# Seven half-size products for the two gates and branch b of a hybrid encoder layer, with the gated sum in natural layout

## The chip, the cores and the metric

The program runs on one core of a Trainium2 chip. A core has a matrix engine (TensorE, here PE, with its weight loads as PEld), a vector engine (DVE), a scalar engine (ACT), a general engine (GpSimd, here POOL) and SyncE (SP), which issues most DMAs. POOL issues the DMAs that add to what lies in the on-chip memory. The metric is the time of one execution in microseconds (us); lower is better.

## The reference

There are two layers on 512 tokens of width 1024, in float32. A layer begins with one input projection of x; its columns are the queries, keys and values of two kinds of attention, a gate g for the second kind, and the two branch gates:

```python
proj = x @ w_in[i]
q_na, k_na, v_na, q_r, k_r, v_r, g_r, gate_a, gate_b = jnp.split(proj, IN_SPLITS, axis=-1)
ya = neighbourhood_attention(q_na.reshape(B, T, NA_HEADS, NA_HEAD_DIM), ...)      # 512 x 512
yb = bidirectional_retention(q_r.reshape(B, T, RET_HEADS, RET_QK_DIM), ..., v_r, g_r, ...)   # 512 x 1024
merged = jax.nn.sigmoid(gate_a) * (ya @ w_branch_a[i]) + jax.nn.sigmoid(gate_b) * (yb @ w_branch_b[i])
y = merged @ w_out[i]
x = layer_norm(DEEPNORM_ALPHA * x + y, ln1_g[i], ln1_b[i])
```

Three of these products concern us: x by gate a's weights, x by gate b's weights, and yb by `w_branch_b`. Each is 512 x 1024 by 1024 x 1024. The layer ends with a gated feed-forward part (`w_up`, a convolution of width 3, `w_down`) with an extra gated input, and a second normalisation.

## The kernel before

**Precision.** Each float32 operand is split into a rounded high part and a low part (`split`: ACT makes the high part, DVE subtracts it to get the low part). A product is three matmuls, high by high, high by low and low by high (`mm3`). So each chunk of weights, 128 x 1024 and 512 KB, costs one ACT cast, one DVE subtraction and the DMA that brings it.

**Weights.** The class `Stream` holds the chunks of both layers in the order of use. `get` hands out the next chunk and prepares (`prep`) those a little ahead; `load` issues the DMAs. Chunks whose split parts are `held` lie in the pool `unit` of 30 buffers (4 KB a partition each), the others in small pools.

**Blocks.** Some products are done by Winograd's scheme: the operands are cut into four quarters, and seven products of half size take the place of eight. The products are called a, c, t1, t2, d, t3 and t4. For t1 to t4 the weights are sums of quarters: a chunk already loaded gets another quarter added, by an accumulating DMA from POOL's queue (`add`), or on POOL with a tensor addition where a quarter is on the chip already (`other`). The activations' sums come from DVE (`vg_sums`: t1, t2, d, t3). One product is 24 matmuls of 512 columns. Before the change, v and g of the retention heads (two blocks, 0 and 1, half of the heads each), the extra input's gate, and the down projection are done in this way.

**Stages of a layer.** In the front part, `vg` runs the fourteen products of blocks 0 and 1, in the order that the tuple `VG` lists, and between them four tiles of gate a (`ga0` to `ga3`) and the first query and key head. Each engine runs the instructions of this part in the order in which they are written. Then follows a middle part, in slots: in each slot `fillers` runs one projection tile from the list `FILL` (24 products of 512 columns with `gemm_t`, output features on the partitions), and steps of retention heads (`RET_AT`) and of neighbourhood attention heads (`NA_AT`) stand in front of it at the slots listed. After `FILL`, `gates` runs eight pairs of tiles: gate b and branch b. In this part a planner orders each engine's instructions, by their place in the text and by when they are ready. Gate a is written to memory after its sigmoid and read again in the next stage. Then come branch a's eight tiles, with the gated sum of both branches, split as it stands because features lie on the partitions already; then the output projection with the first normalisation, the extra input's gate with the up and down projection, and the next layer. In the second layer `plain_x` reads x and applies the last normalisation's factors on DVE.

**Names.** `gt` is a tile of `gemm_t`; `ybt` is branch b's transposed input; `lo`, `hi` are weights' parts; `raw`, `rawa`, `rawd`, `rawt` are chunks as they came; `u`, `v`, `w` are blocks' accumulators; `s`, `sh`, `sl` are sums of activations; `S` is an attention head's scores. In the pinned front part and in most of the later stages, all instructions bear line 84, that of the wrapper that pins them.

```python
for m in range(8):                                            # gates(), before
    sab[m] = unit_f("sab", (P, 2, 512))
    nc.scalar.activation(sab[m][:, 1, :], gemm_t(xs), AF.Sigmoid)
    bb = gemm_t(lambda k: (ybt[k][:, 0, :], ybt[k][:, 1, :]))
    nc.vector.tensor_mul(sab[m][:, 1, :], bb, sab[m][:, 1, :])
```

## Time and profile before

| | |
|---|---|
| median of 3 runs (lowest, highest) | 1700.62 us (1700.49, 1700.91) |
| the profiled execution | 1699.88 us, its span 1697.9 us |
| PE, PEld busy | 1681.9 us, 1404.5 us |
| DVE, ACT, POOL busy | 1207.3 us, 948.7 us, 175.3 us |
| DMA | 250.09 MB, mean 147 GB/s |
| granted TensorE clock | 0.998 |

The span runs from the first to the last instruction; the execution's own time has some 2 us around it. A busy time is the union of an engine's instructions. A row of a group gives the line, the engine, the operation, the tiles (out<-in), the shape and the count, then busy time, the mean length of one in ns, the idle time of the engine in front of them, and what ended that idle time. A row of the timeline or of the chain gives the start and the length in us.

### The profile page before, as it was taken

Reading aid. Unit: us, or ns where it says so; the run is one execution under the profiler, and the core shown is the slowest. Engines: PE = TensorE matmul, PEld = TensorE weight load, DVE = VectorE, ACT = ScalarE, POOL = GpSimd, SP = SyncE. Lnnn points to the kernel's source line nnn. Section 1 sums busy time; section 2 is a strip of 40 time slices with the busy share of each in tenths; the row PEclk is TensorE's granted clock in tenths of the full one; section 3 lists DMA queues with packets and bytes.
Section 4 is the critical chain, followed back from the end, with each engine's and each line's share of the span. In section 5 each row is a group of like instructions: output and inputs, shape, how many; then the busy total and the mean of one; then the engine's idle time right before and its main releaser. Section 6 shows DMA issues by size and latency. Waiting matters only on the chain.

```text
span 1697.9 us, 21017 instructions
## 1 busy us (share of the span) xinstructions
PE 1681.9 (99%) x7895; PEld 1404.5 (83%) x7895; DVE 1207.3 (71%) x1816; ACT 948.7 (56%) x1432; POOL 175.3 (10%) x166
## 2 busy tenths in 40 slices
...
GB/s 322 186 104 131 105 151 123 114 171 126 197 149 145 128 112 162 135 111 173 191 216 149 97 112 124 150 124 108 166 179 198 137 169 124 92 179 131 87 211 99
DMA packets 74406, 250.09 MB, mean 147 GB/s; under 512 B 8640, under 2 KB 9152, under 8 KB 74304
## 3 DMA queue, kind: packets, MB, share of 16 engines
...
## 4 chain that ended last, share of the span: by engine, by line
PE 97%; DVE 2%; ACT 1%; issue 0%; DVEq 0%; ACTq 0%
PE gt L84 32%; PE u L84 13%; PE gt L382 8%; PE gt L381 8%; PE gt L383 8%; PE v L84 7%; PE w L84 3%; PE gn L383 3%; PE gn L382 3%; PE gn L381 3%; PE x L84 2%; PE gn L84 1%; PE na L994 1%; PE pt L982 1%; PE o L383 1%; PE o L382 1%
## 5 line engine op out<-in xcount | busy, mean ns | idle before, releaser
L84 PE MATMUL gt<-x1t,hi 128*128 128x512 f32 x1408 | 433.5, 389 | 0.0
L84 PEld LDWEIGHTS gt<-x1t,hi 128*128 128x128 f32 x1408 | 264.3, 188 | 55.0
L84 PE MATMUL gt<-x1t,lo 128*128 128x512 f32 x704 | 274.1, 389 | 0.1
L84 DVE TENSOR_TENSOR lo<-raw,hi 128x1024 fp32r<-128x1024 f32 (+1 forms) x147 | 182.9, 1253 | 30.5 <-ACT hi L84 30.2
L84 DVE SCALAR_TENSOR_TENSOR ca<-gt,cw,ca 128x511 f32<-128x511 f32 x176 | 131.8, 749 | 79.1 <-ACT ca L84 76.0
L84 ACT CAST hi<-raw 128x1024 fp32r<-128x1024 f32 (+1 forms) x147 | 151.2, 1037 | 32.7 <-PE u L84 14.9
L381 PE MATMUL gt<-xt,hi 128*128 128x512 f32 x416 | 163.5, 393 | 0.0
L382 PE MATMUL gt<-xt,hi 128*128 128x512 f32 x416 | 162.2, 390 | 0.0
L383 PE MATMUL gt<-xt,lo 128*128 128x512 f32 x416 | 162.1, 390 | 0.0
L84 PEld LDWEIGHTS gt<-x1t,lo 128*128 128x128 f32 x704 | 132.1, 188 | 28.2 <-DVE lo L84 1.0
L154 DVE TENSOR_TENSOR lo<-raw,hi 128x1024 fp32r<-128x1024 f32 x72 | 87.9, 1222 | 86.0 <-ACT hi L153 73.7
L84 ACT ACTIVATE ca<-gt,cw 128x512 f32<-128x512 f32 x88 | 68.6, 779 | 131.0 <-PE gt L84 131.0
L153 ACT CAST hi<-raw 128x1024 fp32r<-128x1024 f32 x72 | 75.6, 1051 | 107.0 <-PE gt L382 93.2
L84 DVE TENSOR_TENSOR lo<-rawa,hi 128x1024 fp32r<-128x1024 f32 x90 | 104.5, 1174 | 42.8 <-ACT hi L84 42.6
L84 ACT CAST hi<-rawa 128x1024 fp32r<-128x1024 f32 x90 | 89.6, 1012 | 35.5 <-DMA rawa<-in_wpack 16.9
L383 PEld LDWEIGHTS gt<-xt,lo 128*128 128x128 f32 x416 | 78.1, 188 | 16.6
L381 PEld LDWEIGHTS gt<-xt,hi 128*128 128x128 f32 x416 | 78.2, 188 | 15.1
L382 PEld LDWEIGHTS gt<-xt,hi 128*128 128x128 f32 x416 | 78.2, 188 | 14.6
...
L84 PE MATMUL gt<-xt,hi 128*128 128x512 f32 x192 | 59.4, 391 | 2.7 <-ACT hi L84 2.7
L84 PE MATMUL v<-hi,sa 128*128 128x512 f32 x176 | 56.1, 389 | 0.0
L381 PE MATMUL gn<-hi,mt 128*128 128x512 f32 x128 | 50.1, 392 | 0.0
...
## 6 DMA issues: line engine op xcount, KB each, us to landing
raw<-in_wpack SPq DMA_DIRECT2D x239, 512.0 KB, 3.9
rawa<-in_wpack POOLq DMA_DIRECT2D x58, 512.0 KB, 5.9
lo<-in_wpack POOLq DMA_DIRECT2D x24, 512.0 KB, 6.9
rawa<-in_wpack SPq DMA_DIRECT2D x22, 512.0 KB, 6.4
rawt<-in_wpack SPq DMA_DIRECT2D x22, 512.0 KB, 5.7
rawt<-in_wpack POOLq DMA_DIRECT2D x14, 512.0 KB, 6.6
r_scr<-pp SPq DMA_DIRECT2D x8, 512.0 KB, 9.2
rawd<-in_wpack SPq DMA_DIRECT2D x8, 512.0 KB, 7.0
```

The costliest lines, as they stand in the source:

```text
L84: r = f(*a, **k)
L153: nc.scalar.copy(hi, src)
L154: nc.vector.tensor_sub(lo, src, _f(hi))
L381: nc.tensor.matmul(ps, lh, rh, start=start, stop=False, skip_group_check=more)
L382: nc.tensor.matmul(ps, lh, rl, start=False, stop=False, skip_group_check=more)
L383: nc.tensor.matmul(ps, ll, rh, start=False, stop=stop, skip_group_check=more)
L982: nc.tensor.transpose(ps[:, i * P:(i + 1) * P], S[:, g * 256 + bb * P:g * 256 + (bb + 1) * P], ident)
L994: nc.tensor.matmul(ov[kt], lv, pt[kt // 2][:, sp_, c], start=i == 0 and sp_ == 0, stop=i == 3 and sp_ == 1)
```

## The change

- Gate a and gate b become blocks of seven half-size products, numbers 2 and 3, with tokens on the partitions (natural layout), and run in the front part ahead of and among v's and g's blocks. Both gates are written to memory after the sigmoid (`send`, one product later) and read back as whole rows.
- Branch b becomes such a block (`bb`), in the last seven slots of the middle part. A retention head's transposed output is kept in float32 (`Y`); `quad` and `quad_sums` make the operands, in the buffer that held the transposed x and in units. Its outputs are multiplied with gate b as they come (`M`).
- Branch a is computed in natural layout too; the gated sum is turned by transposes on PE (`turn`) for the output projection.
- On-chip additions on POOL: t2 and t3 of blocks 1, 2 and 3 and t3 of block 0. Branch b's sums are all made by accumulating DMAs.
- The softmax scaling of the attention heads goes from ACT to POOL, and the factors of `plain_x` from DVE to POOL.
- The lists of slots and orders become separate for the two layers.

```diff
-FILL = ("q1", "k1", "ga4", "nq0", "nk0", "q2", "ga5", "k2", "ga6", "nq1", "nk1", "q3", "ga7", "k3", "nq2", "nk2", "nq3", "nk3", "vn")
-RET_AT = (0, 5, 9, 15)
-NA_AT = (17, 19, 21, 23, 25, 27, 30, 32)
+FILL = (('nq0', 'q1', 'nk0', 'k2', 'k1', 'vn', 'q2', 'q3', 'k3', 'nq1', 'nk1', 'nq2', 'nq3', 'nk3', 'nk2'),
+ ('k1', 'q1', 'nk0', 'nk2', 'nq0', 'nq1', 'q2', 'q3', 'k2', 'k3', 'vn', 'nk1', 'nq2', 'nk3', 'nq3'))
+BB = ("a", "c", "t1", "d", "t2", "t3", "t4")
+RET_AT = ((5, 6, 13, 14), (3, 5, 11, 11))
+NA_AT = ((6, 11, 14, 16, 18, 19, 19, 19), (10, 13, 16, 16, 16, 19, 19, 19))
...
-VG0 = ("p0", "p1", "0a", "0c", "1a", "1c", "ga0", "0t1", "ga1", "0t2", "ga2", "0d", "0t3", "1t1", "0t4", "ga3", "1t2", "q0", "1d", "1t3", "k0", "1t4")
-VG1 = ("0a", "0c", "1a", "1c", "ga0", "0t1", "ga1", "0t2", "ga2", "0d", "0t3", "1t1", "0t4", "ga3", "1t2", "q0", "1d", "1t3", "k0", "1t4")
-VG = (VG0, VG1)
+VG = (('p0', 'p1', '2a', '3a', '3c', '2c', '2t1', '2t2', '3t1', '2d', '3t2', '2t3', '3d', '1a', '3t3', '3t4', '2t4', '0a', '0c', '1c', '0t1', '0d', 'q0',
+  '0t2', '1t1', '0t3', '0t4', 'k0', '1d', '1t2', '1t3', '1t4'),
+ ('2a', '2c', '3a', '3c', '3t1', '2t1', '3t2', '2d', '3d', '2t2', '0a', '2t3', '3t3', '0c', '2t4', '1a', 'q0', '0t1', '3t4', '0d', '0t2', '1c', '1t1',
+  '1d', '0t3', '0t4', '1t2', 'k0', '1t3', '1t4'))
+XN_AT = 5
+M_AT = 4
+TABLES_AT = (12, 15)
+REST_AT = (1, 3, 5, 8, 10, 12)
+PEND_AT = (2, 3)
...
+ON_CHIP = ('t3', 't2 t3', 't2 t3', 't2 t3')
+BB_HELD = ('a', 't1', 't2')
+BB_EARLY = 'c'
...
+        def bb_items(l):
+            pos = {(q, j): (l, 44 + 2 * i + j, 0, 1024) for i, q in enumerate("acbd") for j in range(2)}
+            by = {}
+            for it in block_items(pos, {k: up for k in BB_HELD}, BB_EARLY):
+                by.setdefault(it.kind, []).append(it)
+            return [it for k in BB for it in by[k]]
...
-                    for f in FILL:
+                    for f in FILL[l]:
                         self.seq += plain_items(l, f)
-                    for c in (*range(36, 52), *range(60, 72)):
+                    self.seq += bb_items(l)
+                    for c in range(60, 72):
...
+            def block(lh, emit):
+                st = {}
+                def product(kind, ps, first):
+                    for j in range(2):
+                        hi, lo = ws.get()
+                        for i in range(2):
+                            for kk in range(2):
+                                k, r = 2 * j + kk, slice(kk * 512, (kk + 1) * 512)
+                                mm3(ps[i], lh(kind, k, 0, i), lh(kind, k, 1, i), hi[:, r], lo[:, r], first and k == 0, k == 3, not first)
+                def copies(ps, name):
+                    out = [tmp(name) for _ in range(2)]
+                    for i in range(2):
+                        nc.scalar.copy(out[i], ps[i])
+                    return out
+                def corner():
+                    if "t2" in st and "d" in st:
+                        for i, t in enumerate(st["t2"]):
+                            nc.vector.tensor_add(t, t, st["v"][i])
+                            emit(i, 1, t, -1.0)
+                def step(kind):
+                    if kind == "a":
+                        st["u"] = two("u")
+                        product(kind, st["u"], True)
+                        st["p1"] = copies(st["u"], "p1")
+                    elif kind == "c":
+                        w = two("w")
+                        product(kind, w, True)
+                        for i, t in enumerate(st["p1"]):
+                            nc.vector.tensor_add(t, t, w[i])
+                        for i, t in enumerate(st["p1"]):
+                            emit(i, 0, t, 1.0)
+                    elif kind == "t1":
+                        st["v"] = two("v")
+                        product(kind, st["v"], True)
+                        p5 = unit_f("p5", (P, 2, 512))
+                        st["p5"] = [p5[:, i] for i in range(2)]
+                        for i in range(2):
+                            nc.scalar.copy(p5[:, i], st["v"][i])
+                    elif kind == "t2":
+                        product(kind, st["u"], False)
+                        st["t2"] = copies(st["u"], "u2")
+                        corner()
+                    elif kind == "d":
+                        product(kind, st["v"], False)
+                        st["d"] = True
+                        corner()
+                    elif kind == "t3":
+                        product(kind, st["u"], False)
+                        for i, t in enumerate(st["p5"]):
+                            nc.vector.tensor_add(t, t, st["u"][i])
+                            emit(2 + i, 1, t, -1.0)
+                    else:
+                        product(kind, st["u"], False)
+                        for i in range(2):
+                            emit(2 + i, 0, st["u"][i], 1.0)
+                    return st
+                return step
+            stores = []
+            def send():
+                while stores:
+                    g, t, hb, src = stores.pop(0)
+                    nc.sync.dma_start(gscr[g][t * P:(t + 1) * P, hb * 512:(hb + 1) * 512], src)
+            def gate(g):
+                def emit(t, hb, src, sign):
+                    dst = tmp("sg") if hb == 0 and t >= 2 else src
+                    nc.scalar.activation(dst, src, AF.Sigmoid, scale=sign)
+                    stores.append((g, t, hb, dst))
+                return emit
...
+            def vg_emit(hp):
+                def emit(t, hb, src, sign):
+                    (g_tile if hb else v_tile)(hp, t, src)
+                return emit
+                blocks = [block(lh, vg_emit(0)), block(lh, vg_emit(1)), block(lh, gate(0)), block(lh, gate(1))]
...
-            def gate_a(m):
-                sg = tmp("sga")
-                nc.scalar.activation(sg, gemm_t(xs), AF.Sigmoid)
-                nc.sync.dma_start(gscr[m], sg)
...
+                q, kp = h // 2, h % 2
+                Y[q, kp] = unit_f("Y", (P, 2, 2, 256))
                 for dv in range(2):
                     ps = bank("ybt")
                     for t in range(4):
                         nc.tensor.transpose(ps[:, t * P:(t + 1) * P], yb[:, t, dv * P:(dv + 1) * P], ident)
-                    u = unit_r("ybt")
-                    split(u[:, 0, :], u[:, 1, :], ps)
-                    ybt[2 * h + dv] = u
+                    nc.scalar.copy(Y[q, kp][:, dv].rearrange("p a b -> p (a b)"), ps)
...
-                for g in range(4):
-                    nc.scalar.activation(S[:, g * 256:(g + 1) * 256], S[:, g * 256:(g + 1) * 256], AF.Copy, scale=rc[:, g:g + 1])
+                s4 = S.rearrange("p (g n) -> p g n", g=4)
+                nc.gpsimd.tensor_tensor(s4, s4, _ap(rc, 0, [[1, 4], [0, 256]]), ALU.mult)
...
-                        nc.vector.tensor_mul(z, z, g)
-                        nc.vector.tensor_add(z, z, b)
-            def gates():
...
+            def bb():
+                yw = xp.tile([P, 8, 2, 512], F32R, tag="xt", name=nm("yw"))
+                xq = [yw[:, i].rearrange("p a b -> p (a b)").rearrange("p (k c) -> p k c", k=4) for i in range(8)]
+                free = {"a": 0, "c": 2, "t1": 4, "t2": 6}
+                alloc = lambda kind: ((xq[free[kind]], xq[free[kind] + 1]) if kind in free else
+                                      tuple(up.tile([P, 4, 256], F32R, tag="u", name=nm("yq")) for _ in range(2)))
+                X = lambda q, h, kp: Y[q, kp][:, :, h, :]
+                S = {}
+                def quad(kind, q, h):
+                    S[kind] = alloc(kind)
+                    for kp in range(2):
+                        r = slice(2 * kp, 2 * kp + 2)
+                        split(S[kind][0][:, r, :], S[kind][1][:, r, :], X(q, h, kp))
+                sums = quad_sums(X, S, alloc)
+                def load_gate():
+                    for t in range(len(M), len(M) + 2):
+                        M.append(unit_f("M"))
+                        nc.sync.dma_start(M[t], gscr[1][t * P:(t + 1) * P, :])
+                def emit(t, hb, src, sign):
+                    m = M[t][:, hb * 512:(hb + 1) * 512]
+                    nc.vector.scalar_tensor_tensor(m, src, sign, m, op0=ALU.mult, op1=ALU.mult)
+                step = block(lambda kind, k, s, i: S[kind][s][:, k, i * P:(i + 1) * P], emit)
+                quad("a", 0, 0)
+                for n, kind in enumerate(BB):
+                    if n == XN_AT:
                         plain_x()
-                    sab[m] = unit_f("sab", (P, 2, 512))
-                    nc.scalar.activation(sab[m][:, 1, :], gemm_t(xs), AF.Sigmoid)
+                    if n in (0, M_AT):
+                        load_gate()
+                    if n == 1:
+                        quad("c", 1, 0)
+                    if 1 <= n < 5:
+                        next(sums)
+                    if n == 4:
+                        quad("t4", 1, 1)
+                    step(kind)
                     yield
...
-            mt = []
-            for m in range(8):
-                if m % 2 == 0:
-                    wa = ws.get()
-                ba = gemm_t(lambda k: (yat[k][:, 0, :], yat[k][:, 1, :]), nk=4, wt=wa, off=(m % 2) * 512)
-                sa, sb = sab[m][:, 0, :], sab[m][:, 1, :]
-                if m % 4 == 0:
-                    for i in range(m, m + 4):
-                        nc.sync.dma_start(sab[i][:, 0, :], gscr[i])
-                nc.vector.tensor_mul(sa, ba, sa)
-                nc.vector.tensor_add(sa, sa, sb)
-                u = unit_r("mt")
-                split(u[:, 0, :], u[:, 1, :], sa)
-                mt.append(u)
+            mt = {(q, h): [up.tile([P, 4, 256], F32R, tag="u", name=nm("mt")) for _ in range(2)] for h in range(2) for q in range(2)}
+            sa = []
+            for t in range(4):
+                sa.append(unit_f("sa"))
+                nc.sync.dma_start(sa[t], gscr[0][t * P:(t + 1) * P, :])
+            def merge(hb, t, ps):
+                c = slice(hb * 512, (hb + 1) * 512)
+                nc.vector.tensor_mul(sa[t][:, c], ps, sa[t][:, c])
+                nc.vector.tensor_add(sa[t][:, c], sa[t][:, c], M[t][:, c])
+            def turn(hb, t):
+                ps = bank("tr")
+                for k in range(4):
+                    nc.tensor.transpose(ps[:, k * P:(k + 1) * P], sa[t][:, (4 * hb + k) * P:(4 * hb + k + 1) * P], ident)
+                ts = slice((t % 2) * P, (t % 2 + 1) * P)
+                hi, lo = mt[hb, t // 2]
+                split(hi[:, :, ts], lo[:, :, ts], ps.rearrange("p (k c) -> p k c", c=P))
+            for hb in range(2):
+                pss = []
+                for t in gemm_n_tok(lambda k, s, t: yat[k][:, s, t * P:(t + 1) * P], 2, pss, 0):
+                    merge(hb, t, pss[t])
+                    if hb:
+                        turn(0, t)
+            for t in range(4):
+                turn(1, t)
...
-    sga, sgb, sbb, sba = _stat(ga), _stat(gb), _stat(w_bb), _stat(w_ba)
-    for m in range(8):
-        ch += [sgb[m], sbb[m]]
-    ch += list(sga)
-    for m in range(0, 8, 2):
-        ch.append(np.concatenate([sba[m], sba[m + 1]], axis=1))
+    for w in (gb, w_bb, ga, w_ba):
+        ch += list(_mov(w).reshape(-1, P, 1024))
```

209 lines of the change are left out of this document (90 added, 119 removed).

## The prediction

> **What bounds the kernel now.** I read the busy times first, then the chain that ended last, then the order of PE's matmuls, then the busy time by stretch. Times are in us unless marked ns.
>
> ```profile
> PE 1681.9 (99%) x7895; PEld 1404.5 (83%) x7895; DVE 1207.3 (71%) x1816; ACT 948.7 (56%) x1432; POOL 175.3 (10%) x166
> PE 97%; DVE 2%; ACT 1%; issue 0%; DVEq 0%; ACTq 0%
> 99.83 0.39 PE L84 MATMUL u<-lo,sh 128*128 128x512 f32 x1
> 100.06 0.39 PE L84 MATMUL u<-hi,sl 128*128 128x512 f32 x1
> 594.62 87.04 PE gt L84 x384
> ```
>
> The chain that ended last is PE for 97% of the span. A matmul over 512 columns lasts 0.39, but the next starts 0.23 later: 384 of them in a row take 87.04, which is 0.2267 each. That interval, not the 0.39, is what a removed matmul frees. [...]
>
> So PE removed is time removed, as long as the other engines keep up in the stretch where the work stands. By stretch (columns: PE, PEld, DVE, ACT, POOL busy, granted clock, DMA share, GB/s), the front blocks, then the middle (retention, attention, gates and branch b), of layer 0 and of layer 1:
>
> ```profile
> 17.40:129.10 111.70, 109.89 (x482) 89.75 (x481) 89.60 (x110) 70.97 (x96) 29.17 (x17) 1.00 0.61 178
> 129.10:393.30 264.20, 264.20 (x1393) 227.02 (x1392) 157.81 (x327) 178.83 (x317) 16.23 (x20) 1.00 0.48 132
> 857.60:971.50 113.90, 111.42 (x496) 91.26 (x495) 83.20 (x89) 67.93 (x95) 27.25 (x15) 1.00 0.50 147
> 971.50:1235.90 264.40, 264.40 (x1394) 227.21 (x1393) 166.95 (x335) 179.06 (x317) 16.20 (x20) 1.00 0.48 132
> ```
>
> The front has DVE at 80% (89.60 of 111.70) and PE almost gapless; the middle has DVE at 60% (157.81 of 264.20), the reserve that the change spends.
>
> **PE's part of the sum.**
>
> ```profile
> L381 PE MATMUL gt<-xt,hi 128*128 128x512 f32 x416 | 163.5, 393 | 0.0
> L381 PE MATMUL gt<-ybt,hi 128*128 128x512 f32 x128 | 50.0, 391 | 0.0
> 164.00 1.03 PE L882 MATMUL ybt<-ident,yb 128*128 128x128 f32 x8
> 164.79 0.36 PE L381 MATMUL s<-qk,qk 128*128 128x256 f32 x1
> ```
>
> Branch b is 128 steps of three matmuls in two layers, so 192 matmuls a layer; gate a and gate b have the same shape, so 576 a layer in all. Seven products of 24 (2 chunks x 2 token tiles x 2 k-tiles x 3) are 168 a block, 504 for three blocks. Removed: 72 a layer, 144 in all, x 0.2267 = **-32.6**. Branch a keeps its 96 (two halves of 4 tiles x 4 x 3).
> Added: the merged sum is turned, 8 groups of 4 transposes a layer, 64 in all. Eight take 0.79 (164.00 to 164.79), so 64 take **+6.3**. Net PE **-26.3**.
>
> The work also moves. The front loses 4 gate tiles of 24 and gains 14 products: 111.7 + 10 x 5.44 = 166.1. The middle loses 20 tiles and gains 7 products: 264.2 - 13 x 5.44 = 193.5.
>
> **What the other engines pay, middle.**
>
> ```profile
> L154 DVE TENSOR_TENSOR lo<-raw,hi 128x1024 fp32r<-128x1024 f32 x26 | 31.8, 1224 | 41.5 <-ACT hi L153 35.4 <-PE pt L982 5.8
> L154 DVE TENSOR_TENSOR ybt<-ybt,ybt 128x512 fp32r<-128x512 f32 x8 | 5.2, 686 | 3.5 <-ACT ybt L153 3.5
> L1032 DVE TENSOR_TENSOR sab<-gt,sab 128x512 f32<-128x512 f32 x7 | 4.8, 690 | 7.3 <-PE gt L383 7.2
> 42.05 1.27 DVE L84 TENSOR_TENSOR p<-p,w 128x512 f32<-128x512 f32 x2
> L1021 DVE TENSOR_TENSOR xn<-xn,lng 128x1024 f32<-128x1024 f32 x4 | 4.8, 1214 | 0.7 <-DMA xn<-x_scr 0.7
> L153 ACT CAST hi<-raw 128x1024 fp32r<-128x1024 f32 x26 | 27.3, 1051 | 47.1 <-PE gt L382 46.2 <-PE gn L383 0.8
> L974 ACT ACTIVATE S<-S,rc 128x256 f32<-128x256 f32 x32 | 13.6, 498 | 0.5 <-DVE rc L972 0.5
> L1029 ACT ACT_TABLE_LOAD x6 | 7.7, 1283 | 0.1
> L969 ACT ACT_TABLE_LOAD x6 | 7.7, 1283 | 0.1
> L789 ACT ACT_TABLE_LOAD x3 | 3.8, 1283 | 0.1
> L797 ACT ACT_TABLE_LOAD x3 | 3.8, 1283 | 0.1
> L797 ACT ACTIVATE sga<-gt 128x512 f32<-128x512 f32 x4 | 2.4, 596 | 0.0
> ```
>
> DVE loses 20 weight splits x 1.22 = 24.4, 8 products with the gate (5.5) and 8 `ybt` splits (5.5). It gains 14 splits (17.1), 6 adds x 0.64 to 0.69 (4.1), 8 multiplies (5.5), and for branch b's operands 6 low parts, 8 sums and 8 low parts of sums, 22 x 0.69 = 15.2. So 157.8 - 35.4 + 41.9 = 164.3 of 193.5, 85%. In layer 1 the same, since its extra 9 (the eight `xn` operations, 1.21 each) goes to POOL.
> ACT loses 20 casts (21.0), 12 sigmoids x 0.6 (7.2), 8 `ybt` copies (4.7), the softmax scaling (13.6), and nearly all table loads: exponentials and sigmoids no longer alternate, 7.7 + 7.7 + 3.8 + 3.8 less two single loads, some 21. It gains 14 casts (14.7) and 28 copies of half size (about 17). About 143 of 193.5: ACT is no bound, and this part of the change pays.
>
> **POOL against DVE.** The softmax scaling (8 operations of 128x1024 a layer) and layer 1's 8 `xn` operations go to POOL; the front has 14 weight additions there a layer in place of 8. A row of nearest shape prices them:
>
> ```profile
> L84 POOL TENSOR_TENSOR rawa<-rawa,rawd 128x1024 f32<-128x1024 f32 x8 | 23.7, 2966 | 69.6 <-DVE lo L84 69.6
> 53.86 2.70 POOL L84 TENSOR_TENSOR rawt<-rawt,rawd 128x1024 f32<-128x1024 f32 x1
> 56.90 2.91 POOL L84 TENSOR_TENSOR rawt<-rawt,rawd 128x1024 f32<-128x1024 f32 x1
> 54.01 6.96 DVE L84 SCALAR_TENSOR_TENSOR s<-s,xf 128x512 f32<-128x512 f32 x2
> 41.09 6.11 POOL L84 TENSOR_TENSOR rawa<-rawa,rawd 128x1024 f32<-128x1024 f32 x2 [16.21 <-DVE lo L84]
> 61.13 0.39 PE L84 MATMUL u<-hi,sl 128*128 128x512 f32 x1
> 62.62 0.73 PE L84 MATMUL gt<-xt,hi 128*128 128x512 f32 x2 [1.10 <-ACT hi L84]
> L84 DVE TENSOR_TENSOR lo<-raw,hi 128x1024 fp32r<-128x1024 f32 x11 | 17.9, 1629 | 2.5 <-ACT hi L84 2.5
> L84 DVE TENSOR_TENSOR vl<-p,vh 128x512 fp32r<-128x512 f32 x4 | 5.7, 1447 | 0.2
> ```
>
> Two DVE operations that should take 1.3 together took 6.96, ending with the two POOL additions, and PE then waited 1.26 (62.62 - 61.13 - 0.23). The two DVE additions at 42.05, which read PSUM, took their usual time beside POOL's at 41.09. Over the layer-0 front, DVE's excess is 4.5 on `lo<-raw`, 5.6 on `s` and 3.0 on `vl`, about 13 for 8 additions of 2.9: roughly 0.6 of POOL's time returns as DVE time. [...]
> At 0.6, DVE in the middle is 164.3 + 14 = 178 of 193.5 in layer 0 and 192 of 193.5 in layer 1. In the front: 89.6 + 24 splits x 1.22 + 12 adds x 0.68 + 6 x 2.9 x 0.6 = 137.5 of 166.1, 83% against 80%.
>
> **Stalls that I add.**
> - Front, layer 0. The first sum product loses the gate tile ahead of it, so it is due 5.44 earlier.
>
> ```profile
> 39.78 2.35 DVE L84 TENSOR_TENSOR lo<-rawa,hi 128x1024 fp32r<-128x1024 f32 x2
> 45.20 5.44 PE v L84 x24
> ```
>
> Its weights' low parts end at 42.1; it is due at 45.2 - 5.4 = 39.8. Bounds: -1.5 (a stall like that at 61 goes) to +6 (t1 late by 2.3, and t2, now the next product, late by one 2.9 addition). Taken: +3. Layer 1: -2 to +3, taken +1.
> - Middle. Attention's DVE work in the eight heads before, of which these two are the larger:
>
> ```profile
> L964 DVE CUSTOM_DVE_ANT_0 S<-ns,B 128x256 f32<-128x256 f32 x32 | 11.9, 417 | 0.0
> L154 DVE TENSOR_TENSOR pt<-pt,pt 128x512 fp32r<-128x512 f32 x16 | 10.3, 685 | 3.7 <-ACT pt L153 3.6
> ```
>
> They make 2.8 a head, 4.4 with its smaller operations. The lower bound is nothing: DVE has room over the whole stretch. The upper bound comes from the last seven slots alone. They hold bb's products (38.1) and four to five attention heads (transposes and score matmuls, about 14): 52 of PE. DVE there has 14 splits (17.1), 22 operand operations (15.2), 14 adds and multiplies (9.6) and attention (21 for what falls there): 63, plus 4 x 2.9 x 0.6 = 7, so up to 18 late if none of it is done ahead. The weight splits run up to five chunks ahead and the order there is left to the planner, so I take a value near the lower end: +3 in layer 0, +5 in layer 1, where POOL has eight more operations. The transposed x and bb's first operands share one buffer (`xp` has one), so bb's first splits wait for the last tile on x; three attention heads stand there for PE to run. That is inside the same bounds.
> - Turning: the last transposes wait for a multiply and an add (1.4) and a split follows; 48 matmuls on the first half of the merged sum, 10.9, are there to run, but behind them in the text. 0 to 2 a layer, taken +1 each.
> - DMA:
>
> ```profile
> rawa<-in_wpack POOLq DMA_DIRECT2D x58, 512.0 KB, 5.9
> g_scr<-sga SPq DMA_DIRECT2D x16, 256.0 KB, 2.9
> ```
>
> The gates' stores and loads double (before, 16 stores of 256 KB in two layers), and 18 more weight chunks of 512 KB come a layer; the middle has a DMA share of 0.48. SP's queue carries the stores, held back by one product so that they wait for no sigmoid. The eight accumulating loads of bb queue on POOL behind the softmax scaling; that is the third rival. Zero here.
>
> Sum of stalls: 3 + 1 + 3 + 5 + 2 = +14. Total -26.3 + 14 = -12.3. Against the profiled execution's 1699.9 that is 1687.6; the median is 0.7 above that execution, so **1688**.
>
> **Rivals.**
> - Everything is covered. For it: before, PE lost only a few us in gaps although the front's DVE stood at 80%. Time: 1700.6 - 26.3 = 1674.3, up to 5 more.
> - DVE becomes the bound in the middle: the other side. Its place is the last seven slots of each layer's middle, its mechanism POOL holding DVE. With the upper 18 a layer and front and turn as above (6), 1700.6 - 26.3 + 42 = 1716. It decides from the point where the added stalls of a layer pass 13. Against it: work is done ahead in the 141 us before, where DVE has 101.
> - bb's weights come late: each accumulating load lands 5.9 after issue, and one behind a scaling of 2.9 is late by that much. Three late pairs a layer would add 6 x 2.9 = 17 and take the place of the middle's 8: about 1697. Against it: the same four-fold chain of sums runs in the down blocks with a gapless PE.
> - The change does nothing: the stalls come to 26, within 0.2%.
>
> **How the numbers follow.** Forecast (stalls of 5 to 21) 0.50; all covered 0.22; late weights 0.08; DVE bound 0.16; nothing 0.04. A difference under 0.2% (3.4 us) is about what cannot be told from no change. Faster 0.79, same 0.05, slower 0.16. The range takes in the covered case from 1675 and the lower half of the DVE case: 1675 to 1704. The forecast's own range is 1679 to 1696.
>
> **What would show it.** 144 fewer matmuls of 512 columns at 0.227; 64 more transposes; table loads in the middle near none; DVE operations of 3 to 6 us beside POOL's scaling; PE's gaps in the middle in sum under 10. Wrong if PE's gaps are over 26 in sum, or if a DMA stands as their releaser.

## The result, and the profile after

The changed kernel takes 1758.12 us (median of 4 runs, 1757.59 to 1759.28) where the kernel before takes 1700.55: a ratio of 1.0339, 95% interval 1.0321 to 1.0357. It is 58 us slower; 12 faster was forecast. The profiled execution has a span of 1756.3, against 1697.9.

The page: busy times by engine, and the chain that ended last by engine.

```profile
PE 1683.0 (96%) x7815; PEld 1395.4 (79%) x7815; DVE 1316.5 (75%) x1908; ACT 945.4 (54%) x1434; POOL 294.7 (17%) x238
PE 79%; DVE 11%; ACT 4%; DMA 3%; issue 2%; SPq 0%; POOL 0%; DVEq 0%; ACTq 0%; POOLq 0%
```

PE has 80 matmul rows fewer, as forecast (144 removed, 64 added), and yet no less busy time, since matmuls that run slowly count longer (0.79 in place of 0.39 in a row below). PE's share of the chain falls from 97% to 79%, and DVE's rises from 2% to 11%. So PE waits. The waits of PE by releaser (in all, times, longest) say for what; before, the two largest groups came to 2.7 and 1.6 us in all, both on weight parts.

```profile
PE u L96 <- ACT s L96: 9.8, 1, 9.8
PE u L397 <- DVE p L708: 8.5, 1, 8.5
PE v L96 <- ACT hi L96: 7.7, 3, 4.4
PE v L96 <- DVE lo L96: 6.4, 5, 3.2
PE u L96 <- DVE lo L96: 4.0, 2, 2.9
...
PE tr L1211 <- DVE sa L1206: 3.4, 2, 1.7
```

L96 is now the wrapper's line (84 before). Where the waits stand is seen by stage. The rows have the columns of the prediction's windows; they are layer 0's front, middle and branch a's stage, then layer 1's; the last row is a stretch of layer 0's front.

```profile
16.30:204.90 188.60, 169.73 (x721) 137.44 (x720) 132.59 (x148) 112.04 (x149) 56.48 (x35) 0.95 0.70 193
204.90:401.40 196.50, 192.64 (x1057) 165.38 (x1056) 157.49 (x328) 133.51 (x259) 37.93 (x35) 0.99 0.62 152
401.40:435.40 34.00, 31.41 (x155) 25.59 (x153) 27.22 (x40) 12.07 (x19) 0.00 (x0) 1.00 0.42 139
877.80:1061.60 183.80, 168.66 (x713) 135.88 (x711) 131.14 (x123) 101.67 (x140) 52.48 (x31) 0.96 0.60 171
1061.60:1267.30 205.70, 197.96 (x1081) 170.35 (x1081) 156.94 (x327) 139.76 (x266) 45.26 (x39) 0.98 0.62 154
1267.30:1315.50 48.20, 35.19 (x153) 28.24 (x153) 41.14 (x45) 11.83 (x18) 16.20 (x6) 0.86 0.28 98
...
54.00:66.00 12.00, 12.00 (x44) 9.60 (x44) 10.14 (x12) 8.64 (x13) 6.44 (x4) 0.81 1.00 293
```

The fronts were to last 166.1 in layer 0 without stalls and last 188.6; the last stage of layer 1 takes 48.2 for the work that takes 34.0 in layer 0.

I use one more measure, **lost time**: for every two matmuls that follow each other, the distance of their starts less the usual distance (0.2267 for 512 columns; 0.1195 for 256 and 0.1085 for 128, the usual ones in the trace), summed over a stage. It counts gaps and slow matmuls alike. Over the whole span it is 13.1 before and 96.8 after. With the forecast saving of 26.3 on PE this gives 96.8 - 13.1 - 26.3 = 57.4 of the 58.4 by which the span grew.

| lost time, us | front 0 | middle 0 | branch a 0 | front 1 | middle 1 | branch a 1 |
|---|---|---|---|---|---|---|
| before | 2.9 | 1.3 | 0.0 | 3.6 | 1.3 | 0.0 |
| after | 25.4 | 9.8 | 3.3 | 24.3 | 13.5 | 17.5 |

Three stretches of the timeline (start, length, engine, line, operation; in brackets the idle time in front and its releaser) show how the time is lost. The first row is one of the chain of work (start and length of a transfer).

```profile
27.70 17.56 DMA rawd<-in_wpack
...
45.42 4.63 POOL L96 TENSOR_TENSOR rawa<-rawa,rawd 128x1024 f32<-128x1024 f32 x2 [19.02 <-DMA rawd<-in_wpack]
...
47.79 1.04 ACT L96 CAST hi<-rawa 128x1024 fp32r<-128x1024 f32 x1 [8.05 <-POOL rawa L96]
51.78 1.23 ACT L96 ACTIVATE p<-p 128x512 f32<-128x512 f32 x2 [2.94 <-DVE p L96]
52.98 0.62 ACT L96 CAST s<-s 128x512 fp32r<-128x512 f32 x1
...
53.65 0.79 PE L96 MATMUL u<-hi,s 128*128 128x512 f32 x1 [9.78 <-ACT s L96]
...
54.67 1.05 PE L96 MATMUL u<-hi,s 128*128 128x512 f32 x2
55.52 0.63 PE L96 MATMUL u<-lo,s 128*128 128x512 f32 x1
55.95 1.05 PE L96 MATMUL u<-hi,s 128*128 128x512 f32 x2
...
1020.60 2.85 POOL L96 TENSOR_TENSOR rawt<-rawt,rawd 128x1024 f32<-128x1024 f32 x1
1023.39 2.80 POOL L96 TENSOR_TENSOR rawa<-rawa,rawd 128x1024 f32<-128x1024 f32 x1
...
1019.71 4.28 DVE L96 TENSOR_TENSOR vl<-p,vh 128x512 fp32r<-128x512 f32 x2
1023.92 4.49 DVE L96 TENSOR_TENSOR lo<-rawd,hi 128x1024 fp32r<-128x1024 f32 x2
...
1027.33 0.50 PE L96 MATMUL v<-lo,s 128*128 128x512 f32 x1 [3.23 <-DVE lo L96]
...
1265.99 3.34 POOL L1080 TENSOR_TENSOR xn<-xn,lng 128x1024 f32<-128x1024 f32 x1
1269.41 2.68 POOL L1081 TENSOR_TENSOR xn<-xn,lnb 128x1024 f32<-128x1024 f32 x1
1272.05 2.79 POOL L1080 TENSOR_TENSOR xn<-xn,lng 128x1024 f32<-128x1024 f32 x1
1274.92 3.22 POOL L1081 TENSOR_TENSOR xn<-xn,lnb 128x1024 f32<-128x1024 f32 x1
...
1267.04 2.84 DVE L1109 SCALAR_TENSOR_TENSOR M<-u,M 128x512 f32<-128x512 f32 x1
...
1272.57 3.35 DVE L166 TENSOR_TENSOR lo<-rawa,hi 128x1024 fp32r<-128x1024 f32 x1
1275.85 1.27 DVE L708 TENSOR_TENSOR p<-p,u 128x512 f32<-128x512 f32 x2
...
1276.58 0.80 PE L397 MATMUL u<-hi,yq 128*128 128x512 f32 x1 [8.54 <-DVE p L708]
```

- At 43.5 in layer 0's front, t2 of gate a's block follows t1 directly. ACT stands idle for 8.05 in front of one weight cast, because POOL's addition waits for the chunk `rawd`; the activations' sum that PE needs stands behind that cast in ACT's queue. This `rawd` took 17.6 from issue to landing; before, with a tile of gate a between the two products, the two such chunks took 12.0 and 12.6.
- After that gap the matmuls start 0.427 apart in place of 0.2267 (three from 54.67 to 55.95 take 1.28): in the row from 54 to 66 the granted clock is 0.81, and 44 matmuls fill 12 us without a gap, where 53 would fit.
- At 1020 DVE's operations with two inputs on the chip take as long as POOL's additions beside them, or longer: the `vl` operation at 1021.12 takes 2.87 beside an addition of 2.85, the weight split at 1023.92 takes 3.36 beside one of 2.80. The two weight splits take 4.49 in place of 2.4, and PE, 3.23 late, waits for the first.
- At 1267 the same with `plain_x` on POOL: PE needs the bank that DVE must empty after t3 (`p<-p,u`), and the operations ahead of it in DVE's queue take 2.84 and 3.35 in place of 0.69 and 1.22.

### The profile page after: what moved, and what is told of

The parts are those of the page before. It is cut to its first block, busy times and chain, and to the rows that moved or that the text cites. A ratio compares the mean times of both kernels' runs of the same rounds, so it can differ in the third digit from the quotient of the medians.

```text
span 1756.3 us, 21209 instructions
## 1 busy us (share of the span) xinstructions
PE 1683.0 (96%) x7815; PEld 1395.4 (79%) x7815; DVE 1316.5 (75%) x1908; ACT 945.4 (54%) x1434; POOL 294.7 (17%) x238
## 4 chain that ended last, share of the span: by engine, by line
PE 79%; DVE 11%; ACT 4%; DMA 3%; issue 2%; SPq 0%; POOL 0%; DVEq 0%; ACTq 0%; POOLq 0%
PE gt L96 28%; PE u L96 15%; PE v L96 7%; PE w L96 4%; PE gn L398 3%; PE gn L399 3%; PE gn L397 3%; PE gt L399 2%; PE gt L397 2%; PE gt L398 2%; DVE lo L166 2%; DVE lo L96 2%; PE x L96 2%; DVE s L96 1%; ACT hi L96 1%
## 5 line engine op out<-in xcount | busy, mean ns | idle before, releaser
L96 PE MATMUL gt<-x1t,hi 128*128 128x512 f32 x1408 | 433.4, 389 | 0.0
L96 PEld LDWEIGHTS gt<-x1t,hi 128*128 128x128 f32 x1408 | 264.3, 188 | 54.7
L96 PE MATMUL gt<-x1t,lo 128*128 128x512 f32 x704 | 274.1, 389 | 0.1
L96 DVE TENSOR_TENSOR lo<-raw,hi 128x1024 fp32r<-128x1024 f32 (+1 forms) x146 | 174.8, 1206 | 48.5 <-ACT hi L96 48.2
L96 DVE TENSOR_TENSOR lo<-rawa,hi 128x1024 fp32r<-128x1024 f32 x122 | 148.4, 1228 | 72.3 <-ACT hi L96 71.9
L96 DVE SCALAR_TENSOR_TENSOR ca<-gt,cw,ca 128x511 f32<-128x511 f32 x176 | 131.8, 749 | 79.1 <-ACT ca L96 76.0
L96 ACT CAST hi<-raw 128x1024 fp32r<-128x1024 f32 (+1 forms) x149 | 153.0, 1037 | 37.8 <-PE u L96 13.5
L96 PEld LDWEIGHTS gt<-x1t,lo 128*128 128x128 f32 x704 | 132.1, 188 | 28.5 <-DVE lo L96 1.0
L96 ACT CAST hi<-rawa 128x1024 fp32r<-128x1024 f32 x122 | 122.9, 1021 | 52.1 <-DMA rawa<-in_wpack 17.5
L96 ACT ACTIVATE ca<-gt,cw 128x512 f32<-128x512 f32 x88 | 68.6, 779 | 131.4 <-PE gt L96 131.4
L96 POOL DMA_DIRECT2D rawa<-in_wpack x80 | 70.0, 900 | 390.8 <-DVE lo L96 336.6
L96 PE MATMUL u<-hi,s 128*128 128x512 f32 x320 | 105.0, 401 | 11.0 <-ACT s L96 9.8
L96 PE MATMUL v<-hi,s 128*128 128x512 f32 x320 | 106.3, 404 | 9.5 <-ACT hi L96 7.7
L399 PE MATMUL gt<-xt,lo 128*128 128x512 f32 x224 | 87.5, 391 | 1.5 <-DMA lo<-in_wpack 0.8
L397 PE MATMUL gt<-xt,hi 128*128 128x512 f32 x224 | 87.9, 393 | 0.0
L398 PE MATMUL gt<-xt,hi 128*128 128x512 f32 x224 | 87.3, 390 | 0.0
L96 PE MATMUL u<-hi,xt 128*128 128x512 f32 x256 | 81.1, 390 | 3.1 <-DVE p L96 3.1
L96 PEld LDWEIGHTS v<-hi,s 128*128 128x128 f32 x320 | 63.0, 197 | 24.8 <-ACT hi L96 9.0
L96 PEld LDWEIGHTS u<-hi,s 128*128 128x128 f32 x320 | 62.2, 195 | 25.1 <-ACT s L96 10.2
L165 ACT CAST hi<-raw 128x1024 fp32r<-128x1024 f32 x41 | 43.1, 1051 | 57.4 <-PE gn L399 26.0
L96 PE MATMUL v<-lo,s 128*128 128x512 f32 x160 | 65.3, 408 | 6.4 <-DVE lo L96 6.4
L166 DVE TENSOR_TENSOR lo<-raw,hi 128x1024 fp32r<-128x1024 f32 x41 | 50.7, 1237 | 26.6 <-ACT hi L165 26.3
```

Source lines behind the costliest of these rows:

```text
L96: r = f(*a, **k)
L165: nc.scalar.copy(hi, src)
L166: nc.vector.tensor_sub(lo, src, _f(hi))
L397: nc.tensor.matmul(ps, lh, rh, start=start, stop=False, skip_group_check=more)
L398: nc.tensor.matmul(ps, lh, rl, start=False, stop=False, skip_group_check=more)
L399: nc.tensor.matmul(ps, ll, rh, start=False, stop=stop, skip_group_check=more)
```

## The experiments

Each run is one edit of the changed kernel unless said otherwise. First all of them with their measured times, ratios to the kernel before, and lost times by stage; the texts follow. Each ratio's 95% interval is about 0.0016 to either side.

| run | us | ratio | front 0 | middle 0 | branch a 0 | front 1 | middle 1 | branch a 1 |
|---|---|---|---|---|---|---|---|---|
| after | 1758.1 | 1.0339 | 25.4 | 9.8 | 3.3 | 24.3 | 13.5 | 17.5 |
| e1_front_dma | 1744.9 | 1.0262 | 29.6 | 9.1 | 2.2 | 10.6 | 13.5 | 17.4 |
| e2_softmax_act | 1763.5 | 1.0369 | 26.9 | 10.8 | 2.1 | 23.9 | 28.0 | 7.0 |
| e3_xn_dve | 1752.4 | 1.0305 | 26.2 | 9.7 | 3.0 | 24.4 | 13.2 | 11.4 |
| e4_no_pool | 1748.8 | 1.0281 | 29.3 | 13.8 | 2.6 | 9.6 | 18.6 | 11.3 |
| e5_keep_late | 1754.5 | 1.0321 | 20.7 | 9.3 | 2.6 | 24.9 | 13.4 | 17.5 |
| e6_order | 1751.3 | 1.0302 | 19.9 | 14.6 | 3.3 | 18.5 | 12.3 | 17.3 |
| e7_order_plus | 1744.0 | 1.0259 | 18.2 | 14.7 | 3.2 | 17.2 | 14.2 | 11.3 |
| e8_plus_old_order | 1737.1 | 1.0212 | 25.9 | 9.1 | 2.3 | 9.2 | 13.9 | 11.6 |
| e9_no_sums | 1712.3 | 1.0066 | 2.8 | 9.0 | 2.3 | 1.9 | 14.0 | 17.5 |
| e10_xn_later | 1727.0 | 1.0148 | 26.3 | 9.6 | 3.9 | 9.0 | 14.2 | 4.0 |
| e11_pairs | 1733.5 | 1.0191 | 24.9 | 11.0 | 3.9 | 10.1 | 14.6 | 5.5 |
| e12_pairs_dma | 1723.2 | 1.0133 | 17.3 | 11.0 | 3.9 | 10.4 | 13.8 | 5.4 |
| e13_no_pool_sums | 1723.4 | 1.0130 | 14.7 | 9.5 | 2.2 | 1.8 | 14.0 | 16.7 |
| e14_no_dma_sums | 1750.9 | 1.0291 | 23.4 | 9.0 | 2.8 | 18.7 | 14.0 | 17.4 |
| e15_no_bb_sums | 1753.2 | 1.0307 | 25.9 | 8.7 | 2.2 | 25.4 | 8.4 | 18.8 |
| e16_best | 1723.3 | 1.0131 | 14.0 | 10.1 | 3.9 | 10.3 | 14.7 | 5.4 |
| e17_no_scaling | 1757.1 | 1.0327 | 27.5 | 6.0 | 2.5 | 25.2 | 12.9 | 17.6 |
| e18_best_slots | 1720.7 | 1.0113 | 16.6 | 10.3 | 3.9 | 9.5 | 11.1 | 5.8 |

The lost time of a stage whose instructions are the same differs by up to 2 between profiles (middle 0: 9.0 to 9.8 in after, e3, e9, e13 and e14), but by up to 5.6 in front 0: e5, e8 and e10 have the same instructions there and lose 20.7, 25.9 and 26.3. Differences smaller than these are not read as effects.

### Work taken off POOL, part by part

**e1_front_dma**: the front's sums all by accumulating DMA.

```diff
-ON_CHIP = ('t3', 't2 t3', 't2 t3', 't2 t3')
+ON_CHIP = ('', '', '', '')
```

> The 28 weight additions that POOL makes in the two front parts become accumulating DMAs; nothing else changes. Theory P (POOL's operations with two inputs on the chip hold DVE's, and DVE's queue in written order passes the delay on to PE): PE's lost time in the two front parts falls from about 50 us (25.4 and 24.3) to about 20, time about 1728 us. Rival O (the new order asks for t2 and t3 too soon after t1, so their weights are late whoever adds them): the lost time stays at 45 or grows, since a DMA's sum lands 5.9 us after issue where POOL takes 2.9, time 1755 to 1770 us.

**e2_softmax_act**: the softmax scaling on ACT, as before the change.

```diff
-                nc.gpsimd.tensor_tensor(s4, s4, _ap(rc, 0, [[1, 4], [0, 256]]), ALU.mult)
+                for g in range(4):
+                    nc.scalar.activation(S[:, g * 256:(g + 1) * 256], S[:, g * 256:(g + 1) * 256], AF.Copy, scale=rc[:, g:g + 1])
```

> The softmax scaling of the 16 attention heads goes back from POOL to ACT; nothing else changes. P: POOL's 16 scalings of 1.9 us hold DVE for some 10 to 18 us in the two middle parts, and a good part of PE's 23 us lost there (9.8 and 13.5) comes back: about 1750 us. O (the lists of slots crowd DVE and ACT at the end of the middle): ACT gets 27 us of work back in a crowded place, time 1758 to 1768 us.

**e3_xn_dve**: the factors of `plain_x` on DVE, as before the change.

```diff
-                        nc.gpsimd.tensor_tensor(z, z, g, ALU.mult)
-                        nc.gpsimd.tensor_tensor(z, z, b, ALU.add)
+                        nc.vector.tensor_mul(z, z, g)
+                        nc.vector.tensor_add(z, z, b)
```

> The second layer's eight factor operations on x go back from POOL to DVE; nothing else changes. P: the 23 us in which POOL held DVE at the end of the second middle part go, DVE pays 9.7 us for the work itself; PE's 17.5 us lost in the second layer's branch a fall to about 5, time about 1746 us. O: DVE is crowded there, the 9.7 us add to the loss, time 1758 to 1768 us.

**e4_no_pool**: the three edits together.

> All three together: no addition or multiplication of 1024 columns on POOL outside the last stage. P: the gains of the three single ones add up, time about 1705 to 1715 us; what stays over 1675 is not POOL's. O: 1750 us or more.

Measured: e1 gives 13 us back, all of it in layer 1's front (24.3 to 10.6); layer 0's front does not gain (25.4 to 29.6). That is neither theory P's 20 in sum nor rival O's 45. e2 is 5 slower, inside theory O's range: layer 1's middle goes from 13.5 to 28.0 while its branch a stage goes from 17.5 to 7.0, so moving the scaling to POOL was worth it. Its operation lasts 1.94 here, where the prediction took 2.9 from another shape:

```profile
L1035 POOL TENSOR_TENSOR S<-S,rc 128x1024 f32<-128x1024 f32 x16 | 31.0, 1935 | 49.5 <-DVE rc L1033 47.5 <-PE w L399 2.0
```

e3 gives 6 back, in branch a's stage of layer 1 (11.4 stay, where theory P expected 5). e4 gives 9, less than e1 alone, and falls between the two ranges. So taking work off POOL gives time back in two places, layer 1's front and layer 1's branch a stage, but not in layer 0's front, and neither theory alone holds.

### Traffic and order in the front

**e5_keep_late**: four stores of 512 KB moved to a later step of layer 0's front.

```diff
-                at_key(2, ple_keep(l))
+                at_key(9, ple_keep(l))
```

> Layer 0's four stores to r_scr go from step 2 to step 9 of the front part's list; nothing else changes. Theory D (traffic): the 9.9 us gap in front of t2 of block 2 is there because the chunk rawd was issued at 27.7 and landed only at 45.3, while those four stores ran beside it; without them it lands about 5 us earlier, so POOL's addition, ACT's cast and the product follow earlier by that much: PE's lost time in layer 0's front part falls from 25.4 to about 19, time about 1752. Theory O (order): what decides is that t2 follows directly on t1, and the in-order queues give the time back at the next sum: lost time stays within 2 us of 25.4, time 1756 to 1760.

**e6_order**: another list of products, with spacers, in both layers.

```diff
- VG = (('p0', 'p1', '2a', '3a', '3c', '2c', '2t1', '2t2', '3t1', '2d', '3t2', '2t3', '3d', '1a', ...
+ VG = (('p0', 'p1', '2a', '2c', '3a', '3c', '2t1', '1a', '2t2', '2d', '2t3', '3t1', '2t4', '1c', '3t2', '3d', '3t3', '0a', '3t4', '0c', '1t1', 'q0', '1t2', '1d', '1t3', '0t1', ...
```

> Only the list of the front part's products changes: at least one product or one tile on x stands between t1 and t2, and between t3 and t4, of each block, which share an accumulator or a chain of sums. Theory O (order): lost time in the front parts, 25.4 and 24.3, falls to under half, time 1735 or less. Theory P (POOL holds DVE): the same additions hold the same DVE operations, so the lost time moves but stays above 18 in each, time 1750 to 1760.

**e7_order_plus**: e6's list, layer 1's front sums by DMA, `plain_x` on DVE, the stores late. **e8_plus_old_order**: the same with the changed kernel's list.

```diff
-ON_CHIP = ('t3', 't2 t3', 't2 t3', 't2 t3')
+ON_CHIP = (('t3', 't2 t3', 't2 t3', 't2 t3'),
+ ('', '', '', ''))
```

> The list of products with spacers, layer 1's sums in the front part all by accumulating DMA, the last normalisation's factors on DVE, and the four stores at step 9. If the gains add (layer 1's front 14, the factors 6, and whatever the order and the stores give): 1715 to 1735. If the in-order queues limit all of them in the same places, as the run with no POOL additions at all showed (9 in place of 19): 1740 or more.

> As the run before, but with the changed kernel's own list of products, so the difference of the two is the order alone. Layer 1's sums by DMA (-13 when alone) and the factors on DVE (-6 when alone) are in different parts of the program and should add, -19, and the stores give 0 (theory O) to 6 (theory D): 1733 to 1739. If they do not add, above 1742.

Measured: with the four stores moved away, POOL's first addition in e5 starts at 34.8 in place of 45.4, and PE's wait of 9.8 for that sum of activations is 1.8. Front 0 loses 20.7 (theory D expected 19) and the time falls by 3.7. But e8 and e10, with the stores at the same place, have the same short wait and lose 25.9 and 26.3 there. In e10, from 17 to 205, these are the front's two largest waits, and the one for that sum:

```profile
PE v L97 <- ACT p L97: 4.8, 1, 4.8
PE u L97 <- DVE p L97: 4.2, 2, 2.4
...
PE u L97 <- ACT s L97: 1.8, 1, 1.8
```

So the late chunk makes the longest single wait, but without it other waits take its place, and what the stores cost is not shown.

In e6 the spacers take 5 to 6 off each front, not half; in layer 0 that is no more than the spread above, and the middle of layer 0 gives 5 back. Both fronts stay above 18 and the time is in theory P's range. With the sums by DMA the spaced list is worse than the old one in layer 1 (17.2 in e7 against 9.2 in e8). e7's 1744.0 lies where the queues were expected to limit the gains, e8's 1737.1 where they were expected to add. e8 gains 21, where e1, e3 and e5 make 13.3 + 5.7 + 3.7 = 22.7 in sum: with the old list, what is gained in different stages adds.

### The weights' sums left out

Three kernels leave work out, to price it. **e9_no_sums** leaves out all sums of weights in the front's blocks, **e13_no_pool_sums** those that POOL makes, **e14_no_dma_sums** those by accumulating transfer. Each such product then uses one quarter in place of a sum; PE, ACT and DVE do the same work.

```diff
             def add(self, it):
+                if it.block is not None:          # e9
+                    return
                 if it.other is not None:
                     if it.other.raw is None:
                         self.fetch(it.other)
+                    return                        # e13
                     nc.gpsimd.tensor_tensor(it.raw, it.raw, it.other.raw, ALU.add)
                     return
+                if it.block is not None:          # e14
+                    return
                 l, c, o, w = it.plus
```

> The weights' sums of the front part's four blocks are left out, so these products are taken with one quarter in place of two: no addition on POOL and no accumulating transfer there; TensorE, ACT and DVE do the same work as in the changed kernel. Theory W (the weights' sums are the cause, by POOL holding DVE or by the traffic): lost time in the two front parts falls from 25.4 and 24.3 to under 8 each, time 1720 to 1728. Theory O (the products' order and the queues of ACT and DVE are the cause): lost time stays above 16 in each, time 1742 or more.

> The weights' sums that POOL makes in the front part are left out (those products are taken with one quarter fewer); the accumulating transfers stay, and so do all chunks' loads. Theory P (POOL's additions hold DVE): the lost time in the two front parts, 25.4 and 24.3, falls under 10 in each, time 1728 or less. Theory T (traffic: accumulating transfers are late): it stays above 17 in each, time 1745 or more. If both are needed, P holds in layer 1, where all sums by DMA gave 14 back, and in layer 0 some 12 to 17 stay: time 1732 to 1738.

> The reverse: POOL's additions in the front part stay, the accumulating transfers there are left out, and the loads of chunks stay. Theory P: DVE is held as before and the lost time stays above 17 in each front part, time 1745 or more. Theory T: under 10 in each, time 1728 or less. If both are needed, layer 1 stays above 17 and layer 0 falls to 10 to 17: time 1742 to 1750.

The two fronts by window, layer 0 and layer 1, of e9, of e13 and of e14:

```profile
17.20:183.20 166.00, 164.17 (x721) 134.85 (x720) 112.74 (x147) 110.49 (x147) 2.10 (x3) 1.00 0.46 158
854.90:1016.30 161.40, 160.55 (x713) 131.94 (x711) 106.78 (x122) 101.84 (x140) 0.55 (x1) 1.00 0.40 141
```

```profile
17.10:195.00 177.90, 168.72 (x721) 137.65 (x720) 112.98 (x147) 111.03 (x147) 17.81 (x21) 0.97 0.72 201
866.60:1028.00 161.40, 160.54 (x714) 131.98 (x712) 106.54 (x123) 102.00 (x140) 14.44 (x17) 1.00 0.68 195
```

```profile
16.90:203.50 186.60, 170.23 (x721) 137.35 (x720) 135.88 (x147) 110.28 (x147) 42.78 (x17) 0.97 0.41 142
875.40:1053.60 178.20, 165.80 (x714) 134.53 (x712) 126.08 (x122) 101.86 (x139) 38.32 (x15) 0.96 0.36 128
```

Without the sums the fronts lose 2.8 and 1.9, no more than before the change, and 46 us come back. This is theory W's outcome, with a time still below its range. So the sums, with the waits that they bring, make the fronts' whole loss. One thing more differs in e9: a quarter that an on-chip addition needs is no longer fetched ahead of its own turn (the first `rawd` is issued at 44.0 in e9, at 27.7 in the changed kernel), so some early traffic goes too.

In layer 1 the loss needs POOL's additions: 1.8 is left without them, with all accumulating transfers running, and 18.7 of 24.3 without the transfers. In layer 0 the two causes overlap: 14.7 is lost without POOL's additions, 23.4 without the transfers, 2.8 without both. By its lost times e13 is the outcome "both are needed", though its time, 1723.4, is theory P's; e14 is theory P's in all. So POOL's additions alone make nearly the whole loss of layer 0's front and most of layer 1's, and the transfers alone about half of layer 0's.

Leaving an addition out takes away both its hold on DVE and the wait for the sum itself, and these runs do not separate the two. That the hold is there shows in DVE's busy time: 132.59 with POOL's additions and 112.74 without, for 148 and 147 operations; 131.14 and 106.78 in layer 1. The 28 additions take 78.2 on POOL (16 of 2754 ns and 12 of 2894), and 44.2 of it returns as DVE time, a share of 0.57.

### The factors behind the drain, and the blocks in step

**e10_xn_later**: e8 with `plain_x` one product later, behind the drain of t3.

```diff
-XN_AT = 5
+XN_AT = 6
```

> As the run with layer 1's sums by DMA, the factors on DVE and the stores late, and the factors' eight operations now stand one product later, behind the drain of t3. Theory Q (the queue): the 6.3 us gap in front of branch b's last product is DVE working off six of the eight operations ahead of the second drain; it goes, and the branch stage's lost time falls from 11.6 to about 5, time about 1731. Rival R: DVE is short of time there in any order, and the operations hold up the gated sum instead: lost time stays above 9, time 1735 to 1738.

In e8, DVE's queue at that place (timeline) had seven of the eight factor operations between the two halves of the drain:

```profile
1253.00 0.68 DVE L709 TENSOR_TENSOR p<-p,u 128x512 f32<-128x512 f32 x1
1253.60 1.22 DVE L1082 TENSOR_TENSOR xn<-xn,lnb 128x1024 f32<-128x1024 f32 x1
1254.73 2.35 DVE L1081 TENSOR_TENSOR xn<-xn,lng 128x1024 f32<-128x1024 f32 x2
...
1262.15 0.69 DVE L709 TENSOR_TENSOR p<-p,u 128x512 f32<-128x512 f32 x1
```

and in e10 both halves run together:

```profile
1254.01 1.28 DVE L709 TENSOR_TENSOR p<-p,u 128x512 f32<-128x512 f32 x2
```

The stage's lost time falls from 11.6 to 4.0, the time by 10, of which this is 7.6. This is theory Q's outcome. This stage of layer 1 lost 14.2 more than layer 0's; e3 and e10 account for 13.7 of it, 6.1 by taking the factors off POOL and 7.6 by the queue's order.

**e11_pairs**: e10 with layer 0's gate blocks in step, and **e12_pairs_dma**: in step in both layers, all sums by DMA.

```diff
+ VG = (('p0', 'p1', '2a', '2c', '3a', '3c', '2t1', '3t1', '2d', '2t2', '3d', '3t2', '2t3', '3t3', '2t4', '3t4', '0a', '0c', '1a', '1c', '0t1', 'q0', '0t2', '0d', '1t1', ...
```

> As the run before, and in layer 0 the gates' two blocks run in step, each product of the one followed by the same product of the other, so that a whole product stands between two that share an accumulator or a chain of sums. If the sums asked for too soon are the cause in layer 0's front part: lost time there falls from about 21 to 26 to under 14, time about 10 less than the run before. If traffic at the cold start or POOL is: 18 or more, and the time of the run before within 4.

> The blocks in step in both layers, and all sums by accumulating DMA. Against the run before, layer 0's front part differs by POOL against DMA alone: if POOL's additions hold DVE there, its lost time falls by 5 or more; if traffic limits it, it grows by 3 or more. Layer 1's front part differs by the order alone from the 9.2 us measured with DMA: 5 to 13 expected, since no order there has shown itself better than the changed kernel's own.

A whole product between neighbours does nothing for layer 0's front while POOL adds there (24.9 against 26.3). e11 is also 6.4 slower than e10, outside the 4 expected; the table's stages account for 3.0 of that, and the rest is open. DMA in POOL's place did nothing in layer 0's front with the old order (29.6 in e1). Both together bring it to 17.3, and to 14.0 and 16.6 in e16 and e18 below, which have the same instructions there. e12 was expected to gain 5 or more there if POOL's additions hold DVE, and gains 7.6. So in layer 0 the additions and the order have to go together, and 14 to 17 stay with the sums by DMA, as 14.7 did in e13.

### The middle

**e15_no_bb_sums** leaves out the sums of branch b's weights, **e17_no_scaling** the softmax scaling.

```diff
+                if it.bb:                         # e15, in add
+                    return
-                nc.gpsimd.tensor_tensor(s4, s4, _ap(rc, 0, [[1, 4], [0, 256]]), ALU.mult)      # e17
```

> The weights' sums of branch b's block (eight accumulating transfers a layer) are left out; the rest is the changed kernel. The prediction's third rival (branch b's weights late on POOL's queue) expects the middle's lost time, 9.8 and 13.5, to fall by 5 or more in each layer, time 1748 or less. Theory L (the last slots hold more work for DVE and ACT than PE's 52 us cover, and the heads' chains wait their turn there): within 2 of the changed kernel in each middle, time 1754 to 1760.

> The softmax scaling of the attention heads is left out, so POOL does none and holds no DVE operation by it, and each head's chain is one step shorter; the rest is the changed kernel. The prediction's second rival (POOL holding DVE makes DVE the bound in the middle): the middle's lost time falls from 9.8 and 13.5 to under 6 in each, time about 1746. Theory L: DVE's and ACT's own work in the last slots remains, the lost time falls by under 4 in each, time 1750 to 1757.

e15 takes 5.1 off layer 1's middle and 1.1 off layer 0's, so late weights are a cause in layer 1 alone. e17 takes 3.8 off layer 0's and 0.6 off layer 1's, under 4 in each as theory L expected. Even the 3.8 need not be a hold on DVE, since each head's chain is a step shorter too. The hold by the scaling is small, as the two middles of e17 show beside the changed kernel's rows above:

```profile
208.00:400.70 192.70, 190.97 (x1057) 164.32 (x1056) 152.02 (x328) 133.09 (x259) 22.36 (x27) 1.00 0.63 155
1061.20:1266.20 205.00, 197.28 (x1080) 170.26 (x1080) 155.50 (x327) 139.89 (x266) 30.07 (x31) 0.98 0.61 154
```

DVE's busy time falls from 157.49 to 152.02 and from 156.94 to 155.50. That is 6.9 of the 31.0 that the scaling takes on POOL, a share of 0.22, where the weights' additions return 0.57. Neither rival is the cause of the greater part of the two middles' 23.3.

### The remedies together

**e16_best**: all sums by DMA, layer 0's blocks in step, the changed kernel's list in layer 1, the factors on DVE behind the drain, the stores late. **e18_best_slots**: the same, with layer 0's slots in layer 1's middle.

```diff
-RET_AT = ((5, 6, 13, 14), (3, 5, 11, 11))
-NA_AT = ((6, 11, 14, 16, 18, 19, 19, 19), (10, 13, 16, 16, 16, 19, 19, 19))
+RET_AT = ((5, 6, 13, 14), (5, 6, 13, 14))
+NA_AT = ((6, 11, 14, 16, 18, 19, 19, 19), (6, 11, 14, 16, 18, 19, 19, 19))
```

> The remedies together: all weights' sums by DMA, the factors on DVE behind t3, the stores late, the blocks in step in layer 0, the changed kernel's own list in layer 1. If each stage keeps what it had (layer 0's front part 17, layer 1's 9, the middles 10 and 14, the branch stages 4 each): 1720 to 1724, still slower than before by 20. If the stages were lucky draws of the transfers' timing: above 1727.

> As the run before, with layer 0's lists of slots (projection tiles, retention, attention) in layer 1 too. Theory L (what the middle loses comes from the work standing in the last slots): layer 1 has five of eight attention heads start at slot 16 or later in its own list and three in layer 0's less crowded one, so layer 1's middle falls from 14 to layer 0's 9 to 11, time 3 to 5 less. If it is branch b's own chain of operand splits: unchanged within 1.

(The lists have six heads from slot 16 on in layer 1 and five in layer 0, not five and three.) The gains hold together: 1723.3, as expected. Other slots take 3.6 off layer 1's middle, which speaks for theory L, though no run separates the slots from the rest of that theory; what else the middles lose stays open. The best version, 1720.67, is 37 us faster than the changed kernel and still 1.13% slower than the kernel before (interval 0.96% to 1.30%). Its windows, fronts and then middles:

```profile
16.40:190.80 174.40, 164.73 (x698) 132.65 (x696) 110.03 (x143) 105.06 (x141) 28.88 (x33) 0.97 0.90 242
870.40:1039.40 169.00, 163.59 (x713) 132.62 (x711) 106.20 (x122) 101.34 (x140) 26.78 (x31) 0.99 0.86 229
190.80:393.20 202.40, 197.44 (x1080) 168.64 (x1081) 160.55 (x332) 138.98 (x266) 38.85 (x36) 1.00 0.61 151
1039.40:1242.60 203.20, 198.87 (x1080) 169.79 (x1081) 160.10 (x332) 139.35 (x266) 38.78 (x36) 0.99 0.62 152
```

With DMA in POOL's place the fronts' DMA share is 0.90 and 0.86, and DVE is back at 110 and 106. This points to the transfers as what limits the fronts now; no run takes them out of this version. The fronts now lose 26.1, 19.6 more than before, against 4 x 5.44 = 21.8 of PE time that the gates' blocks save: 2.2 is left over. The middles and branch a's stages lose 31.1, 28.5 more than before, against 2 x 5.44 - 6.3 = 4.6 that branch b's blocks save after the turning. That part does not pay here as it stands. e9 says the same from the other side: even with the fronts' sums left out the changed kernel takes 1712.3, 0.66% more than the kernel before.

## Why the prediction was wrong

- **PE's part was right.** 80 matmul rows fewer; layer 0's front lasts 166.0 in e9 where 166.1 was worked out. The -26.3 is in the result: lost time and this saving together give 57.4 of the 58.4 by which the span grew. The stalls are what failed: +14 was taken, and the six stages of the table lose 84.7 more than before.
- **Front, +3 and +1: the step that failed.** Measured: +22.5 and +20.7. The bounds -1.5 to +6 came from one event, the first sum products and their two weight halves, with t2 late by one addition of 2.9; PE waited 9.8 there, because the addition itself waited for its chunk. All later additions were priced at nothing: the front has fourteen a layer on POOL, and each can hold what DVE does next or be late itself. Without the fronts' sums the loss is gone (2.8 and 1.9 in e9). The prediction had the mechanism and its size (0.6 of POOL's time; 0.57 measured), but put it into an average: DVE at 83% of 166.1, so it fits. (The two held operations that it read as ending with POOL's additions end 1.2 after them, 60.97 against 59.81; no term hangs on that.) DVE's busy time was even a little less (132.6 against 137.5). An average share does not bound a wait in a queue worked off in written order: what stands behind a held operation is late at once, however idle the engine is later. The weight split at 1023.92 that held PE up for 3.23 is such a case.
- **DMA, zero: failed in layer 0.** The mean share in the front, 0.70, hides the burst at the start: `rawd` took 17.6 in place of 12.0, and POOL's, ACT's and PE's queues stood behind it (9.8). What the four stores beside it cost is open (e5). Without POOL's additions, 11.9 of layer 0's lost time goes with the accumulating transfers and the early fetches (14.7 in e13 less 2.8 in e9); in layer 1 nothing does (1.8 and 1.9).
- **Middle, +3 and +5.** Measured +8.5 and +12.2, inside the bounds of 0 to 18 and well above the values taken. DVE's busy time there is 157.5 and 156.9, less than the 178 and 192 worked out. One term in that sum was too large: 14 a layer for the scaling, at 0.6 of 2.9 for each of eight; an operation takes 1.94, and DVE's busy time falls by 5.5 and 1.4 without it (e17). No DVE operation beside it takes over 3 (the longest 2.92, at 357.33), against the forecast sign of 3 to 6. Late weights (third rival) are 5.1 of the lost time in layer 1, and leaving the scaling out (second rival) gives 3.8 back in layer 0; the greater part is open.
- **Turning, +1 each.** PE waits 3.4 in all for the last gated sums, 1.7 each: near.
- **The factors on POOL** were counted as DVE time inside the middle. They run at the end of branch b's block, ahead of the drain that empties the bank PE needs next. That stage of layer 1 lost 14.2 more than layer 0's, and no term stood for it: 6.1 goes with the factors off POOL, 7.6 with their place in the queue (e3, e10).
- **The rival on the other side** (DVE held by POOL, 1716) had the right mechanism in the wrong place: it put it into the last slots of the middle, where leaving the scaling out gives back 3.8 and 0.6, not into the fronts and branch a's stage. The sentence "wrong if PE's gaps are over 26 in sum" is what happened: PE is idle for 73 of the 1756.3.
- **Not in the sum at all**: after seven of the changed kernel's eight gaps over 2.5 us, PE runs at nearly half pace for a few us, 0.427 between starts in place of 0.2267; after the gap at 43.5 for 12 matmuls or 5 us. Of the 96.8, matmuls about 0.43 apart make some 14 (3.4 and 1.4 in layer 0's front and middle; 5.6, 0.4 and 3.0 in layer 1's front, middle and branch a stage). Shorter gaps had such stretches behind them too, as told below.
